# A mark set one granule later, and softmax portions counted twice, in a hybrid decoder block

## The chip, the cores and the metric

The kernel runs on one core of a Trainium2 chip. The metric is the device time of one execution in microseconds (us). Five instruction queues matter here: TensorE (PE, with its weight loads shown apart as PEld), VectorE (DVE), ScalarE (ACT), GpSimd (POOL) and SyncE (SP), which issues nearly all DMA transfers. Each queue runs its instructions in order; an instruction waits on semaphores for other engines.

## The reference

One decoder layer over 256 positions of 2048 channels in float32. The first half mixes three branches, the second is a gated feed-forward network.

```
h = rms_norm(x);  proj = h @ w_in            # a_in, b_in, q, kv, gates, merge gates
y_a = conformer_conv(a_in)                   # GLU, depthwise conv of 31, LayerNorm, swish, proj
y_b = chunked_spatial_gating(b_in)           # gelu, LayerNorm, 8 triangular 128x128 mixes, proj
y_c = native_sparse_attention(q, kv, gates)  # three attentions, see below, proj
mixed = (g_a * y_a + g_b * y_b + g_c * y_c) @ w_o
x = x + rms_norm(mixed)
h = rms_norm(x);  u = causal_dwconv3(h @ w_up)
x = x + rms_norm((silu(u_g) * u_v) @ w_down)
```

The sparse attention has 16 query heads in 4 groups, and three branches, each with keys and values of its own, added under gates:

```
kc = compress_blocks(k_cmp, pe_k, w1_k, w2_k)   # 15 blocks of 32 positions, a small MLP each
vc = compress_blocks(v_cmp, pe_v, w1_v, w2_v)
p_cmp = masked_softmax(q @ kc)                  # compressed branch: 15 keys
o_cmp = p_cmp @ vc
o_slc, o_win = ...                              # at 256 positions both see all earlier positions
o = gate0 * o_cmp + gate1 * o_slc + gate2 * o_win
```

## The kernel before

Every large product is made in three passes from a high and a low part of each operand. A weight piece of 128x1024 (512 KB) is fetched by SP into `wraw` (5 buffers, L106); ACT copies it rounded into `whi` (L146), and DVE subtracts to get `wlo` (L147), 4 buffers each. A *granule* is two such pieces. `mm_t` (L195 to L197) issues the three matmuls for one block of 128 input channels and 128 positions.

TensorE's main line is written in program order. The stage around the change is `branch(0, ...)`, the projection of the gating branch B: for each of four column blocks `cb` it makes the merge gates `pg` from four granules of `wt_g` (96 matmuls), evicts them through ACT as `mg` (Tanh, L1019), then makes `py` from two granules of `wt_p` (`q` is 0 and 1; 24 matmuls each, with `Bt` as the other operand), and DVE multiplies both into `mac` (L1044). `branch(1, ...)` does the same for branch A, with `At`.

Everything else runs in the background. Generators stand in a queue `bg`; `pump(ns)` is called after each granule, adds `ns` (6500 in this stage) to a running debt, and takes steps of the first generator while the debt is positive. Each step's `yield` says how many ns it is reckoned to cost.

```
    def pump(ns):
        debt[0] = min(debt[0], 0.0) + ns if not bg else debt[0] + ns
        while bg and debt[0] > 0:
            try:
                debt[0] -= next(bg[0])
            except StopIteration:
                bg.popleft()
```

So the yields decide only between which granules an operation is issued. A scheduler then places the instructions of each engine, by priorities and by its own reckoning of time, so that operations of one pump can move past neighbours.

In the queue, in this order, stand: the layer norm of branch A (`lna_gen`, which writes `At`, L514 to L520); `cmp_prep(0)`, which builds the compressed keys' operand `bk` (steps `bt`, L601, on DVE; L605 on ACT; L606 on DVE); `hold("outputs")`, which yields 6000 at each step until the mark "outputs" is set; `cmp_gen(0)`, the compressed keys: first product `zp` (L617, L619: 32 matmuls on four pieces of `w1`), then `hp` (L628) and `kcp` (L640); `cmp_prep(1)` and `cmp_gen(1)`, the same for the values, ending in `vcp` (L654) and `vbd` (L656); `cmp_attn(0)` and `cmp_attn(1)`, one compressed softmax for each half of the positions; and `attn`, eight attention units of the selected and window branches (scores `s`, transposes `pp`, values `O`).

`cmp_attn` issues scores `sc` (L716, PE), a masked softmax `ce` on DVE with one Exp on ACT (L727 to L739), in portions of 800, 800, 1300 and 100, and then a transpose `pcp` (L743, PE), copied out by ACT as `pct` (L745). The first attention units take `pct` at L825.

The mark "outputs" is set in `branch(0)` at `cb == 1`, after the first of the two `py` granules, just ahead of that granule's pump.

Of the kernel before, what the change touches and what calls it, by code (L numbers as in the profile page):

```python
# [56 lines left out]
def block(ctx: ExitStack, tc: tile.TileContext, x, xf, fp, cst, rows, sgw, w1, w2, wf_a, wt_bv, wf_bu, wf_c,  # L57
# [8 lines left out]
    marks = set()  # L66
# [12 lines left out]
    def bank(shape, name):  # L79
        return PB["pool"].tile(shape, F32, tag="bg", name=name)  # L80
# [7 lines left out]
    bg = deque()  # L88
    debt = [0.0]
# [8 lines that stand above are left out]
# [52 lines left out]
    def granule(src):  # L150
        return [piece(src[:, a:a + 1024], 1024) for a in (0, 1024)]
# [42 lines left out]
    def mm_t(ps, xh, xl, hi, lo, first, last):  # L194
        PE.matmul(ps, lhsT=xh, rhs=hi, start=first, stop=False)  # L195
        PE.matmul(ps, lhsT=xh, rhs=lo, start=False, stop=False)  # L196
        return PE.matmul(ps, lhsT=xl, rhs=hi, start=False, stop=last).ins  # L197

    def until(name):

        while name not in marks:
# [4 lines that stand above are left out]
# [43 lines left out]
    def q1(name, shape=(128, T)):  # L249
        return P1.tile(list(shape), F32, tag="q", bufs=12, name=name)  # L250
# [458 lines left out]

    Ct_box = {}  # L710

    def cmp_attn(qt):
        ps = bank([128, 2, 4, 2, 16], f"sc{qt}")
        for gg in range(2):
            for j in range(4):
                PE.matmul(ps[:, gg, j].rearrange("p r n -> p (r n)"), lhsT=qf[:, gg * 4 + j, qt * 128:qt * 128 + 128],  # L716
                          rhs=kcb[:, gg], start=True, stop=True)
        e = q1(f"ce{qt}", (128, 16, 16))
        psf = ps.rearrange("p g j r n -> p (g j r) n")
        m = P1.tile([128, 16], F32, tag="cm", name=f"cm{qt}")  # L720

        def bc(a):
            return a[:, None, :].to_broadcast([128, 16, 16])

        def bi(a):
            return a[:, :, None].to_broadcast([128, 16, 16])
        V.tensor_add(e, psf, bc(cs[:, K_CA + qt * 16:K_CA + qt * 16 + 16]))  # L727
        V.reduce_max(m, e, axis=AX.X)
        yield 800
        V.tensor_sub(e, e, bi(m))  # L730
        S.activation(e, e, AF.Exp)
        V.tensor_mul(e, e, bc(cs[:, K_C1 + qt * 16:K_C1 + qt * 16 + 16]))
        yield 800
        V.reduce_sum(m, e, axis=AX.X)
        V.tensor_scalar(m, m, TINY, None, op0=ALU.max)
        V.reciprocal(m, m)
        m4 = m.rearrange("p (g j r) -> p g j r", g=2, j=4)
        V.tensor_mul(m4, m4, gsg[:, qt, 0:16].rearrange("p (g r j) -> p g j r", g=2, r=2))
        V.tensor_mul(e, e, bi(m))  # L739
        yield 1300  # L740
        pp = bank([128, 2, 128], f"pcp{qt}")
        for gg in range(2):
            PE.transpose(pp[:, gg], e[:, gg * 8:gg * 8 + 8].rearrange("p a n -> p (a n)"), ident)  # L743
        pct[qt] = q1(f"pct{qt}", (128, 2, 128))
        S.activation(pct[qt], pp, AF.Copy)  # L745
        yield 100
# [127 lines left out]
            yield from u.values(O)  # L874

    for qt in range(2):
        bg.append(cmp_attn(qt))

    def alloc_C():
        Ct_box["t"] = s16(P1, [128, 8, 2, T], R, "Ct")  # L880
# [119 lines left out]
    def branch(bi, act_of):  # L1000

        for cb in range(4):
            pg = [PS.tile([128, 512], F32, tag="acc", name=f"pg{bi}{cb}{t}") for t in range(2)]
            for q in range(4):
                hs = granule(wt_g[(bi * 4 + cb) * 4 + q])
                for k in range(4 * q, 4 * q + 4):
                    hi, lo = hs[(k % 4) // 2]
                    c = slice((k % 2) * 512, (k % 2) * 512 + 512)
                    for t in range(2):
                        ts = slice(t * 128, t * 128 + 128)  # L1010
                        mm_t(pg[t], hT[:, k, 0, ts], hT[:, k, 1, ts], hi[:, c], lo[:, c], k == 0, k == KT - 1)
                if q < 3:
                    pump(BUDGET)
            tgs = {}
            for t in range(2):
                for a in range(2):
                    tgs[t, a] = q1(f"mg{bi}{cb}{t}{a}")
                    with tc.high_priority(offset=int(PR)):
                        gated[0] = S.activation(tgs[t, a], pg[t][:, a * 256:a * 256 + 256], AF.Tanh,  # L1019
                                                scale=rh[:, t:t + 1]).ins  # L1020
            marks.add("gates")
            pump(BUDGET)
            py = [PS.tile([128, 512], F32, tag="acc", name=f"py{bi}{cb}{t}") for t in range(2)]
            for q in range(2):
                hs = granule(wt_p[(bi * 4 + cb) * 2 + q])
                if cb == 0 and q == 0:
                    until("BA"[bi])
                act = act_of()
                for k in range(4 * q, 4 * q + 4):
                    hi, lo = hs[(k % 4) // 2]  # L1030
                    c = slice((k % 2) * 512, (k % 2) * 512 + 512)
                    for t in range(2):
                        ts = slice(t * 128, t * 128 + 128)
                        pe_last[0] = mm_t(py[t], act[:, k, 0, ts], act[:, k, 1, ts], hi[:, c], lo[:, c], k == 0, k == 7)
                if q == 0:
                    if cb == 1:
                        marks.add("outputs")
                    pump(BUDGET)
            for t in range(2):
                for a in range(2):  # L1040
                    cc = slice(cb * 512 + a * 256, cb * 512 + a * 256 + 256)
                    y = mac[:, t, cc] if bi == 0 else tgs[t, a]
                    with tc.high_priority(offset=int(PR)):
                        V.scalar_tensor_tensor(y, tgs[t, a], 1.0, py[t][:, a * 256:a * 256 + 256], op0=ALU.add,  # L1044
                                               op1=ALU.mult)
                        if bi:
                            V.tensor_add(mac[:, t, cc], mac[:, t, cc], y)
            pump(BUDGET)

    def mix_gen(cb):  # L1050

        for j in range(2 * cb, 2 * cb + 2):
# [10 lines left out]
            if j < NG:  # L1063
# [3 lines left out]
                mix["a", j] = a  # L1067

    branch(0, lambda: Bt_box["t"])
    branch(1, lambda: At)  # L1070
    until("A")
    until("C")
# [19 lines left out]
    for cp in range(2):  # L1092
# [20 lines left out]
        for n in range(2):  # L1113
            cb = 2 * cp + n
# [552 lines left out]
```

## Time and profile before

| | us |
|---|---|
| median of 3 runs | 1583.37 |
| lowest, highest | 1582.46, 1584.4 |
| the profiled execution's own time | 1584.43 |
| its span in the profile | 1582.7 |
| TensorE busy in the span | 1562.7 |
| VectorE busy | 1291.0 |
| ScalarE busy | 911.7 |

The profile is of one execution. A line of the timeline or of a group gives the start and duration, the engine, the source line, the operation, the tile written and the tiles read; a bracket at its end gives the idle time of that engine just before it and what released it. TensorE's matmuls overlap, so what one costs is read from one start to the next. The granted clock is 1.00 when TensorE runs at full speed.

### The profile page before, as it was taken

Reading aid. Unit: us, or ns where it says so; the run is one execution under the profiler, and the core shown is the slowest. Engines: PE = TensorE matmul, PEld = TensorE weight load, DVE = VectorE, ACT = ScalarE, POOL = GpSimd, SP = SyncE. Lnnn points to the kernel's source line nnn. Section 1 sums busy time; section 2 is a strip of 40 time slices with the busy share of each in tenths; the row PEclk is TensorE's granted clock in tenths of the full one; section 3 lists DMA queues with packets and bytes.
Section 4 is the critical chain, followed back from the end, with each engine's and each line's share of the span. In section 5 each row is a group of like instructions: output and inputs, shape, how many; then the busy total and the mean of one; then the engine's idle time right before and its main releaser. Section 6 shows DMA issues by size and latency. Waiting matters only on the chain.

```text
span 1582.7 us, 22435 instructions
## 1 busy us (share of the span) xinstructions
PE 1562.7 (99%) x8146; PEld 1325.7 (84%) x8146; DVE 1291.0 (82%) x2210; ACT 911.7 (58%) x1465; POOL 18.2 (1%) x46
## 2 busy tenths in 40 slices
PE   9999999998999999999999999999999999999997
PEld 7888899887777777888888888888888888888885
DVE  7899999878764554878887988888777777799898
ACT  7544544466476575556465655565555555556563
POOL 1000020000000000000000000000000000000000
PEclk9999999999999999999999999999999999999999
DMA  9555566666444546665784666666666666766672
GB/s 374 187 190 184 186 179 208 196 186 206 160 140 144 167 142 195 186 198 187 239 273 150 204 193 190 188 188 192 189 188 188 187 193 192 229 209 214 199 274 86
DMA packets 85440, 307.95 MB, mean 195 GB/s; under 512 B 9808, under 2 KB 10832, under 8 KB 84304
## 3 DMA queue, kind: packets, MB, share of 16 engines
q1 hardware_dynamic: 83952, 301.91, 60.1%
q0 software_dynamic: 944, 4.19, 0.8%
q8 instruction: 64, 1.05, 0.3%
q10 hardware_dynamic: 432, 0.41, 0.1%
q14 instruction: 48, 0.39, 0.1%
HBM read 301.23 MB, written 4.19 MB: 193 GB/s over the span
## 4 chain that ended last, share of the span: by engine, by line
PE 94%; DVE 3%; ACT 1%; issue 1%; DMA 0%; DVEq 0%; SPq 0%; ACTq 0%
PE ps L175 29%; PE ps L182 15%; PE pd0b L936 5%; PE pd1a L936 4%; PE pg L196 3%; PE pg L197 3%; PE pg L195 3%; PE py L196 3%; PE py L195 3%; PE py L197 2%; PE poa L936 2%; PE pg1a L936 2%; PE pg0a L936 2%; PE pd0a L936 2%; PE pd1b L936 1%; PE po L197 1%
## 5 line engine op out<-in xcount | busy, mean ns | idle before, releaser
L147 DVE TENSOR_TENSOR wlo<-wraw,whi 128x1024 fp32r<-128x1024 f32 (+1 forms) x376 | 457.1, 1218 | 98.7 <-ACT whi L146 92.0
L146 ACT ACTIVATE whi<-wraw 128x1024 fp32r<-128x1024 f32 (+1 forms) x376 | 393.5, 1052 | 153.2 <-PE pg L197 61.1
L175 PE MATMUL ps<-h2T,whi 128*128 128x512 f32 x1360 | 325.0, 391 | 0.0
L175 PEld LDWEIGHTS ps<-h2T,whi 128*128 128x128 f32 x1360 | 249.8, 188 | 48.2
L182 PEld LDWEIGHTS ps<-h2T,wlo 128*128 128x128 f32 x1360 | 174.5, 191 | 6.7
L182 PE MATMUL ps<-h2T,wlo 128*128 128x256 f32 x1360 | 176.6, 283 | 0.0
L175 PE MATMUL ps<-hT,whi 128*128 128x512 f32 x640 | 157.4, 392 | 0.0
L217 ACT ACTIVATE t<-ps 128x256 f32<-128x256 f32 x125 | 47.6, 382 | 187.0 <-PE ps L175 186.6
L901 DVE TENSOR_TENSOR wlowraw<-wraw,whiwraw 128x1024 fp32r<-128x1024 f32 x90 | 108.8, 1223 | 38.7 <-ACT whiwraw L901 37.2
L175 PEld LDWEIGHTS ps<-hT,whi 128*128 128x128 f32 x640 | 116.0, 189 | 21.2
L901 ACT ACTIVATE whiwraw<-wraw 128x1024 fp32r<-128x1024 f32 x90 | 94.7, 1057 | 49.2 <-PE py L197 17.4
L218 DVE TENSOR_TENSOR t<-ps,t 128x256 f32<-128x256 f32 x125 | 52.8, 423 | 70.3 <-ACT t L217 69.8
L478 DVE SCALAR_TENSOR_TENSOR cv<-hb,fps,cv 128x256 f32<-128x256 f32 x240 | 105.1, 479 | 0.2 <-ACT cv L474 0.2
L196 PE MATMUL pg<-wlo,hT 128*128 128x512 f32 x256 | 101.1, 395 | 0.4 <-DVE wlo L147 0.2
L197 PE MATMUL pg<-whi,hT 128*128 128x512 f32 x256 | 100.5, 393 | 0.0
L195 PE MATMUL pg<-whi,hT 128*128 128x512 f32 x256 | 98.7, 393 | 0.0
L182 PEld LDWEIGHTS ps<-hT,wlo 128*128 128x128 f32 x640 | 84.7, 190 | 4.7
L182 PE MATMUL ps<-hT,wlo 128*128 128x256 f32 x640 | 86.8, 283 | 0.0
L196 PEld LDWEIGHTS pg<-wlo,hT 128*128 128x128 f32 x256 | 48.1, 188 | 12.1 <-DVE wlo L147 1.2
L197 PEld LDWEIGHTS pg<-whi,hT 128*128 128x128 f32 x256 | 48.1, 188 | 10.3 <-issue 0.7
L195 PEld LDWEIGHTS pg<-whi,hT 128*128 128x128 f32 x256 | 47.9, 188 | 10.4 <-issue 0.7
L1388 ACT ACTIVATE fa<-fs,fps 128x256 f32<-128x256 f32 x88 | 52.5, 596 | 1.1 <-DVE fs L220 0.9
(1334 smaller groups left out, 2797.0 us busy)
## 6 DMA issues: line engine op xcount, KB each, us to landing
wraw<-in_wf_up_dram SPq DMA_DIRECT2D x176, 512.0 KB, 4.3
wraw<-in_wt_g_dram SPq DMA_DIRECT2D x64, 512.0 KB, 4.3
wraw<-in_wt_p_dram SPq DMA_DIRECT2D x48, 512.0 KB, 4.3
wraw<-in_wt_dn_dram SPq DMA_DIRECT2D x48, 512.0 KB, 4.4
wraw<-in_wf_a_dram SPq DMA_DIRECT2D x32, 512.0 KB, 4.4
wraw<-in_wt_gp_dram SPq DMA_DIRECT2D x20, 512.0 KB, 4.1
wraw<-in_wt_dq_dram SPq DMA_DIRECT2D x20, 512.0 KB, 4.5
qa<-in_wt_dq_dram SPq DMA_DIRECT2D x20, 512.0 KB, 4.1
```

Of the source, the lines that this page charges most:

```text
L146: S.activation(hi[:, :n], raw[:, :n], AF.Copy)
L147: V.tensor_sub(lo[:, :n], raw[:, :n], hi[:, :n].bitcast(F32))
L175: ins = PE.matmul(ps[:, :, ts], lhsT=ws[k // 8][0][:, c:c + 128], rhs=mov[:, k, :, ts], start=(k == 0 and not t), stop=(k == n - 1), skip_ ...
L182: ins = PE.matmul(ps[:, 1, ts], lhsT=ws[k // 8][1][:, c:c + 128], rhs=mov[:, k, 0, ts], start=False, stop=False, skip_group_check=True).ins
L195: PE.matmul(ps, lhsT=xh, rhs=hi, start=first, stop=False)
L196: PE.matmul(ps, lhsT=xh, rhs=lo, start=False, stop=False)
L197: return PE.matmul(ps, lhsT=xl, rhs=hi, start=False, stop=last).ins
L218: V.tensor_add(t1 if rb is not None else dst, ps[:, 0], t1)
L478: V.scalar_tensor_tensor(ca[:, j], hb[:, j, k:k + T], w(j, k), ca[:, j], op0=ALU.mult, op1=ALU.add)
L901: seq[eng] = [op(*args, **kw).ins]
L936: ins = PE.matmul(bank, lhsT=a[x], rhs=w[y], start=first and j == 0, stop=last and j == 2).ins
L1388: S.activation(a, s, AF.Identity, bias=fps[:, C_FB + f:C_FB + f + 1], scale=w[2])
```

## The change

Two edits, in the stage of `branch(0)`. The mark "outputs" is set after both `py` granules of `cb == 1` and not after the first, so that `hold` lets `cmp_gen(0)` start at the next pump, which comes behind the second granule. And each `cmp_attn` is wrapped in `apart`, which passes on its steps with twice the reckoned cost, so that one pump takes about half as much of them. No operation on the chip is added, dropped or changed in shape. Lines behind the new helper move down by 5.

```diff
     Ct_box = {}
 
+    def apart(work):
+
+        for ns in work:
+            yield 2.0 * ns
+
     def cmp_attn(qt):
...
     for qt in range(2):
-        bg.append(cmp_attn(qt))
+        bg.append(apart(cmp_attn(qt)))
...
                 if q == 0:
-                    if cb == 1:
-                        marks.add("outputs")
                     pump(BUDGET)
+            if cb == 1:
+                marks.add("outputs")
             for t in range(2):
                 for a in range(2):
                     cc = slice(cb * 512 + a * 256, cb * 512 + a * 256 + 256)
```

## The prediction

> **What bounds the kernel now.** I read the page first, then TensorE's waits, then the two places they point to.
>
> ```profile
> span 1582.7 us, 22435 instructions
> PE 1562.7 (99%) x8146; PEld 1325.7 (84%) x8146; DVE 1291.0 (82%) x2210; ACT 911.7 (58%) x1465; POOL 18.2 (1%) x46
> PE 94%; DVE 3%; ACT 1%; issue 1%; DMA 0%; DVEq 0%; SPq 0%; ACTq 0%
> ```
>
> TensorE sets the time: busy for 99% of the span, 94% of the chain. An edit that moves background work can only win where PE stands still or runs slowly, and can only lose by making it do so elsewhere. TensorE's own waits (engine, line, awaited: us in total, times, longest):
>
> ```profile
> PE zp L617 <- DVE bk L606: 4.0, 1, 4.0
> PE pcp L743 <- DVE ce L739: 3.0, 1, 3.0
> PE s L758 <- ACT pct L745: 0.5, 1, 0.5
> ```
>
> These three are nearly all of its waiting in mid-kernel, and they are what the edits move: zp is the compressed keys' first product, pcp the transpose that ends a compressed softmax, s the scores behind it. Windows of 1 us show what follows each wait (columns: length, busy time and count of PE, PEld, DVE, ACT and POOL, then the granted clock, DMA share, GB/s):
>
> ```profile
> 369.00:370.00 1.00, 1.00 (x6) 1.00 (x6) 0.50 (x2) 1.00 (x1) 0.14 (x2) 0.50 0.79 127
> 371.00:372.00 1.00, 1.00 (x11) 1.00 (x10) 0.51 (x2) 1.00 (x2) 0.00 (x0) 1.00 0.52 205
> 430.00:431.00 1.00, 1.00 (x7) 1.00 (x6) 1.00 (x9) 0.00 (x0) 0.00 (x0) 0.50 0.00 0
> 432.00:433.00 1.00, 1.00 (x7) 0.87 (x7) 1.00 (x7) 0.07 (x1) 0.00 (x0) 1.00 0.00 0
> ```
>
> After either wait PE works at a granted clock of 0.50, and is back at 1.00 by 371 and by 432. So each stall costs its idle time and a slow stretch. TensorE's timeline prices both:
>
> ```profile
> 362.65 0.39 PE L197 MATMUL py<-whi,Bt 128*128 128x512 f32 x1
> 367.08 0.58 PE L617 MATMUL zp<-whi,bk 128*128 128x256 f32 x1 [4.04 <-DVE bk L606]
> 370.61 0.28 PE L617 MATMUL zp<-whi,bk 128*128 128x256 f32 x1
> 372.50 0.63 PE L195 MATMUL py<-whi,Bt 128*128 128x512 f32 x2
> 377.99 1.00 PE L628 MATMUL hp<-sel,zs 128*128 128x64 f32 x8
> 378.79 0.71 PE L195 MATMUL pg<-whi,hT 128*128 128x512 f32 x2
> 385.31 0.33 PE L640 MATMUL kcp<-hid,w2s 128*128 128x64 f32 x2
> 403.20 1.87 PE L716 MATMUL sc<-kcb,qf 128*128 128x32 f32 x16
> 417.06 0.38 PE L743 MATMUL pcp<-idn,ce 128*128 128x128 f32 x2
> 417.27 1.87 PE L716 MATMUL sc<-kcb,qf 128*128 128x32 f32 x16
> 418.98 0.48 PE L195 MATMUL py<-whi,Bt 128*128 128x512 f32 x1
> 425.65 0.69 PE L743 MATMUL pcp<-idn,ce 128*128 128x128 f32 x2 [3.00 <-DVE ce L739]
> 426.81 2.08 PE L758 MATMUL s<-kkv,qf 64*128 64x128 f32 x16 [0.47 <-ACT pct L745]
> 432.11 0.48 PE L195 MATMUL pg<-whi,hT 128*128 128x512 f32 x1
> 436.61 1.16 PE L758 MATMUL s<-kkv,qf 64*128 64x128 f32 x16
> 437.70 0.50 PE L196 MATMUL pg<-wlo,hT 128*128 128x512 f32 x1
> 478.14 1.05 PE L825 MATMUL O<-pct,vbd 128*128 128x128 f32 x8
> 479.03 1.04 PE L816 MATMUL pp<-idn,ep 128*128 128x128 f32 x8
> ```
>
> Start-to-start prices at full clock: a granule of 24 py matmuls 377.99 - 372.50 = 5.49 us (0.229 each), a zp matmul (372.50 - 370.61) / 16 = 0.118, hp 0.80, sc 1.71, pcp 0.21, s 437.70 - 436.61 = 1.09, O for one group 0.89. The first 16 zp took 370.61 - 367.08 = 3.53 where 1.89 would do: the slow clock cost 1.64. From pcp to 432.11 there are 6.46 us, less the wait of 0.47 is 5.99, for 0.21 + 1.09 + 2 x 0.89 = 3.08 of work: 2.91 lost. So stall one is worth 4.04 + 1.64 = 5.7, stall two 3.00 + 0.47 + 2.91 = 6.4. No edit here can win much over 12 us.
>
> **Edit one: the mark "outputs" a granule later.** In the changed program's order of instructions the first 24 py matmuls of the second granule now stand ahead of the zp products, where before they stood behind them; no matmul is added. The weight splits of that granule take the places in the DVE and ACT queues that the zp weights had; SP fetches them in the new order too. The reason for the wait stays on DVE:
>
> ```profile
> 366.27 0.42 DVE L520 SCALAR_TENSOR_TENSOR At<-lz,At 128x256 fp32r<-128x256 f32 x1
> 366.60 0.76 DVE L606 TENSOR_TENSOR bk<-bt,bk 128x256 fp32r<-128x256 f32 x2
> 367.27 1.23 DVE L147 TENSOR_TENSOR wlo<-wraw,whi 128x1024 fp32r<-128x1024 f32 x1
> 368.74 0.76 DVE L606 TENSOR_TENSOR bk<-bt,bk 128x256 fp32r<-128x256 f32 x2
> 374.61 2.30 DVE L601 TENSOR_SCALAR bt<-kd,fps 128x60 f32<-128x60 f32 x12
> 376.81 1.23 DVE L147 TENSOR_TENSOR wlo<-wraw,whi 128x1024 fp32r<-128x1024 f32 x1
> 380.27 1.42 DVE L1044 SCALAR_TENSOR_TENSOR mac<-mg,py 128x256 f32<-128x256 f32 x4
> ```
>
> PE's last py before the wait starts at 362.65, so the granule runs from 362.88 to 368.37; bk's first two pieces land at 367.36, under it. The 4.04 us are covered and the clock stays up. What is late next is DVE: no row here has an idle time in brackets. From start to start an At takes 0.33, a wlo with an At 368.74 - 367.27 = 1.47, so a wlo 1.14; a bk pair 0.67; a bt 2.20 / 12 = 0.18; mac x4 about 1.33, its 1.42 less the 0.09 by which a next one overlaps. Its queue in the new order, after the bk pair that starts at 368.74: third zp split at 369.41 (lands 370.64); mac x4, fourth zp split at 371.88 (373.11); two pg splits (374.25, 375.39); a zp split for the values, 11 bt, another, 5 bt; then the split for pg's second granule at 380.52 (381.75). PE against it: 16 zp to 370.26, one more, wait 0.26; the group and one more zp to 371.58, two pg to 372.04, wait 1.07; 7 zp to 373.94, wait 0.31; 22 pg to 379.3, hp to 380.1, two pg to 380.55, wait 1.20; 22 pg to 386.79, kcp. New waits: 2.84 us in four pieces. Before, kcp came at 385.31 with 24 matmuls fewer behind it, which is 390.80 on the same footing. Edit one gains 4.0. (As a sum: 4.04 + 1.64, plus 1.03 of small losses between 378.79 and 385.31, where 24 matmuls took 6.52 instead of 5.49, less 2.84: 3.9.) Bounds: no DVE lag, 6.7; a lag twice as long, 1.0.
>
> **Edit two: softmax portions counted double.** No operation is added or removed; the yields weigh twice, so cmp_attn and all behind it in the queue spread over one more pump, and the order shows: 44 matmuls between sc(0) and pcp(0) (53 before), 32 between sc(1) and pcp(1) (15 before), then 18 more before s.
>
> ```profile
> 403.89 2.15 DVE L656 SCALAR_TENSOR_TENSOR vbd<-vcp,cs 128x128 f32<-128x128 f32 x8
> 425.17 0.42 DVE L739 TENSOR_TENSOR ce<-ce,cm 128x256 f32<-128x256 f32 x1
> 426.66 1.56 ACT L1019 ACTIVATE mg<-pg,rh 128x256 f32<-128x256 f32 x4
> L146 ACT ACTIVATE whi<-wraw 128x1024 fp32r<-128x1024 f32 (+1 forms) x376 | 393.5, 1052 | 153.2 <-PE pg L197 61.1
> ```
>
> The chain sc(1) to pcp(1) took 425.65 - 418.98 = 6.67 us of DVE and ACT behind 15 matmuls, 15 x 0.229 = 3.4 us. Now 32 matmuls give 7.3 us, and the order takes two wlo splits (2.3) out of the chain and puts mac x4 (1.33) in; ce's last step (425.17, 0.42) would be done some 1 to 2 us before PE asks. So pcp(1) is covered; pct is covered by the 18 matmuls behind it. In front of pcp(0) 44 matmuls, 10.1 us, stand against a chain like pcp(1)'s with the eight vbd ahead of it, 6.67 + 2.15 = 8.8. Who is delayed: mg x4 now stands right behind pct(0) on ACT, and the next pg needs the PSUM that mg's first two read. Since the last py, PE has pcp and sc to do, 1.92 us; ACT has a split (1.05), pct and two mg (1.56 / 4 = 0.39 each, pct taken as one), 2.2, and some 0.25 of handing over: PE waits about 0.55 us. Edit two gains 3.00 + 0.47 + 2.91 - 0.55 = 5.8. Bounds: with pcp(1) still late by half, 3; with the mg wait hidden, 6.4.
>
> **What is moved behind both.** The eight attention units start two pumps later and end 27 matmuls later, with 38 matmuls (8.7 us) still ahead of the next stage, so nothing of it hangs over. I put this at nothing: matmuls cover it.
>
> ```profile
> 440.00:500.00 60.00, 60.00 (x306) 46.83 (x305) 33.57 (x93) 41.49 (x111) 0.00 (x0) 1.00 0.52 158
> ```
>
> PE never waits in these 60 us, and DVE and ACT have 26 and 18 us free.
>
> **Sum.** 3.9 + 5.8 = 9.7 us. The profiled execution took 1584.43 (span 1582.7 and 1.7 around it), 1.06 over the median 1583.37 of the three runs; 9.7 off that median is 1573.7.
>
> [...] Half clock stood after an idle of 3.00 us (425.65). [...]
>
> **The rivals.**
> *The slow stretch belongs to the work, not the gap.* If 425.65 to 432.11 ran slowly because those are small matmuls, it stays slow when moved: gain 9.7 - 2.9 = 6.8, 1576.6. [...] Against it: s ran in 1.09 at 436.61, full clock. 5%.
> *The DVE lag is enough to slow the clock.* Four waits in 11 us might drop it as one of 4 us does; a slow stretch at half clock costs 1.6 (first) to 2.9 (second). Gain 6.8 to 8.1; 1576. Against it: no single wait is over 1.2 us. 8%.
> *One stall stays.* If pcp(1) is as late as before relative to PE, only edit one gains: 3.9, 1579.5. 4%.
> *It does not do what it says*, the lag eats edit one and the mg wait grows: no difference, 1583. 4%.
> *Slower: attention waits on its single pair of PSUM banks.* Scores and transposes of a unit share one two-bank buffer, so each transpose group waits for ACT's weights and each score group for ACT's eviction. If the two pumps push units into stretches where ACT also has mg and the splits, each of 8 units could hold PE. It decides from (9.7 + 3.2) / 8 = 1.6 us a unit; at 2 us a unit, 16 - 9.7 = 6 us slower, 1589.5. Against it: the 60.00 of 60 above, and ACT's free 18 us. 11%.
>
> **How the numbers follow.** Likeliest: both stalls go, 68%, 1573.7, its own range 1571 (no lag) to 1576.5 (lag twice as long). Taking in the two clock cases brings in 81%, less the tails of each; I go on to 1579.5 for the stall that stays, and down to 1570.8. Outside are the no-change and slower cases and thin tails. About 0.2%, 3.2 us, can be told from no change here: faster 68 + 5 + 8 + 4 = 85%, within 4%, slower 11%.
>
> **What would show it.** In the new trace: PE's waits no longer name bk or ce; instead about four waits for wlo, 2 to 3.5 us in sum, near 370 to 382; granted clock 1.00 from 360 to 440; pcp(1) without a wait; a short wait of pg for mg near 418; the first pg behind O some 10 us earlier than the old 432.11 plus 50 matmuls. I am wrong if a wait over 2.5 us stands between 360 and 440, or if PE idles in the attention units.

## The result and the profile after

The changed kernel takes 1574.71 us (median of 5 runs, 1574.34 to 1575.46), the kernel before 1583.37 (5 runs, 1582.46 to 1584.4): a ratio of 0.9947, 95% interval 0.9932 to 0.9961, or 8.7 us less. The forecast was 1573.7. The profiled execution took 1574.36, its span is 1572.7. The head of its page:

```profile
span 1572.7 us, 22434 instructions
PE 1558.4 (99%) x8146; PEld 1322.0 (84%) x8146; DVE 1289.9 (82%) x2210; ACT 911.2 (58%) x1465; POOL 18.2 (1%) x46
```

The span is 10.0 us shorter at the same 8146 matmuls; PE's busy time fell by 4.3 us, since matmuls at half clock count as longer (a zp matmul 0.41 us before, at half clock, and 0.28 at full). TensorE's waits, all of the view:

```profile
PE warm L287 <- POOL wz L284: 1.4, 1, 1.4
PE zp L619 <- DVE wlo L147: 1.0, 2, 0.8
PE pg L196 <- DVE wlo L147: 0.8, 1, 0.8
PE pv L401 <- ACT swraw L117: 0.4, 1, 0.4
PE pg L195 <- ACT mg L1024: 0.3, 1, 0.3
PE pd1a L941 <- DVE wloq_4b L906: 0.2, 1, 0.2
```

No wait names bk, ce or pct any more; in their place stand short waits for weight splits and one for mg. From L712 on the new kernel's lines are 5 higher: pcp is L748, s L763, O L830. The rows of TensorE's timeline that answer to those of before:

```profile
367.89 0.28 PE L617 MATMUL zp<-whi,bk 128*128 128x256 f32 x1
370.33 0.39 PE L619 MATMUL zp<-wlo,bk 128*128 128x256 f32 x1 [0.26 <-DVE wlo L147]
372.79 0.38 PE L619 MATMUL zp<-wlo,bk 128*128 128x256 f32 x1 [0.78 <-DVE wlo L147]
381.39 0.50 PE L196 MATMUL pg<-wlo,hT 128*128 128x512 f32 x1 [0.82 <-DVE wlo L147]
386.51 0.33 PE L640 MATMUL kcp<-hid,w2s 128*128 128x64 f32 x2
418.56 0.50 PE L195 MATMUL pg<-whi,hT 128*128 128x512 f32 x1 [0.27 <-ACT mg L1024]
426.00 0.38 PE L748 MATMUL pcp<-idn,ce 128*128 128x128 f32 x2
430.44 1.16 PE L763 MATMUL s<-kkv,qf 64*128 64x128 f32 x16
431.53 2.05 PE L830 MATMUL O<-pct,vbd 128*128 128x128 f32 x16
433.34 0.47 PE L196 MATMUL pg<-wlo,hT 128*128 128x512 f32 x1
```

The first zp and pcp(1) have nothing in brackets; s takes 1.09 from start to start and both O groups 1.81, the prices of full clock. The first pg behind O starts at 433.34 where before it stood at 432.11 with 50 matmuls still to come: 432.11 + 50 x 0.229 = 443.56, so 10.2 us earlier, where some 10 were forecast. Two windows hold the two places:

```profile
370.00:380.00 10.00, 8.92 (x49) 7.32 (x49) 10.00 (x26) 5.60 (x10) 0.00 (x0) 1.00 0.85 284
420.00:430.00 10.00, 10.00 (x47) 8.20 (x46) 6.76 (x17) 3.88 (x5) 0.00 (x0) 1.00 0.27 92
```

Granted clock 1.00 in both: the slow stretches went with the stalls. Not all of the 10.0 us of span is the change's: the anchor rows lie 0.4 to 0.5 us earlier than before already ahead of the first edited instruction (the py that would follow 362.65 starts at 362.88 before; here 24 py matmuls, 24 x 0.229 = 5.49, precede 367.89, so it starts at 362.40). The medians' 8.7 is the fairer number.

### The profile page after: what moved, and what is told of

Same layout as the page of the kernel before. It is cut to its first block, busy times and chain, and to the rows that moved or that the text cites. A ratio compares the mean times of both kernels' runs of the same rounds, so it can differ in the third digit from the quotient of the medians.

```text
span 1572.7 us, 22434 instructions
## 1 busy us (share of the span) xinstructions
PE 1558.4 (99%) x8146; PEld 1322.0 (84%) x8146; DVE 1289.9 (82%) x2210; ACT 911.2 (58%) x1465; POOL 18.2 (1%) x46
## 4 chain that ended last, share of the span: by engine, by line
PE 94%; DVE 3%; ACT 1%; issue 1%; DMA 0%; DVEq 0%; SPq 0%; ACTq 0%
PE ps L175 29%; PE ps L182 15%; PE pd0b L941 5%; PE pd1a L941 4%; PE pg L197 3%; PE pg L196 3%; PE pg L195 3%; PE py L196 3%; PE py L195 3%; PE py L197 3%; PE poa L941 2%; PE pg1a L941 2%; PE pg0a L941 2%; PE pd0a L941 2%; PE pd1b L941 1%; PE po L195 1%
```

## The experiments

**One edit at a time.** The prediction gave each edit a gain of its own, 4.0 and 5.8. But in the order of instructions only the two together put more work ahead of pcp(1): between sc(1) and pcp(1) stand 15 matmuls before, none with the mark alone, 15 with the weight alone, 32 with both. The mark alone:

```diff
-        bg.append(apart(cmp_attn(qt)))
+        bg.append(cmp_attn(qt))
```

> Only the mark is set a granule later; the softmax portions count as before. Theory A (the prediction's sum: two edits, each worth its own stall): the zp stall and its slow clock go as in the changed kernel, pcp(1) stays as it was, gain 4.0 us, about 1579.4. Theory B (the edits work only together, since what covers pcp(1) is how many matmuls fall between the two halves of the second softmax): in this kernel's order no matmul at all stands between sc(1) and pcp(1), where the kernel before had 15, so the wait there grows from 3.0 us to about 4.5 (the chain took 4.9 us in the changed kernel, with 1.3 of it for mac, which is not in it here) and the clock falls after it: gain 4.0 - 1.5 = 2.5, about 1580.9. A wait of 3.0 at pcp would speak for A, one over 4 for B.

It took 1582.06 us (11 runs), ratio 0.999, interval 0.9981 to 0.9999: 1.4 us gained. Two of its waits, and rows of its timeline:

```profile
PE zp L619 <- DVE wlo L147: 1.0, 2, 0.8
PE pcp L748 <- DVE ce L744: 4.3, 1, 4.3
```

```profile
423.20 0.69 PE L748 MATMUL pcp<-idn,ce 128*128 128x128 f32 x2 [4.31 <-DVE ce L744]
424.37 2.08 PE L763 MATMUL s<-kkv,qf 64*128 64x128 f32 x16 [0.47 <-ACT pct L750]
426.38 3.60 PE L830 MATMUL O<-pct,vbd 128*128 128x128 f32 x16
```

Stall one is gone, as forecast. Stall two has grown from 3.00 to 4.31 us, since no matmul is left to cover the second softmax: some 3.4 us of cover are gone (15 x 0.229), while the softmax on DVE lost two weight splits (2.3 us) from its middle. And s and O still run slowly: s took 2.01 us from start to start (424.37 to 426.38) for the 1.09 of full clock, and the granted clock was 0.50 from 422.83 to 429.66. With the mark worth some 3 us (below) and a wait 1.3 longer, 1.7 would be left; 1.4 was measured.

The weight alone:

```diff
                 if q == 0:
+                    if cb == 1:
+                        marks.add("outputs")
                     pump(BUDGET)
-            if cb == 1:
-                marks.add("outputs")
```

> Only the softmax portions count double; the mark is set where it was. Theory A: pcp(1) is covered, the zp stall of 4.0 us stays, gain 5.8 us, about 1577.6. Theory B: the order has the same 15 matmuls between sc(1) and pcp(1) as before, so both stalls stand as they were: no difference, 1583.4, with waits of 4.0 at zp and 3.0 at pcp.

It took 1583.65 us (11 runs), ratio 1.0, interval 0.9991 to 1.0009: nothing. Its two large waits:

```profile
PE zp L617 <- DVE bk L606: 4.0, 1, 4.0
PE pcp L748 <- DVE ce L744: 3.0, 1, 3.0
```

Both old stalls, to the tenth. One edit gained 1.4, the other nothing, both 8.7: the split of the sum into 4.0 and 5.8 was wrong.

**What edit two needs.** Is the mark itself needed for stall two, or only a pump boundary inside the second softmax, wherever it comes from? With the mark where it was and a weight of 2.5, the order puts 57 matmuls between sc(1) and pcp(1):

```diff
-            yield 2.0 * ns
+            yield 2.5 * ns
...
                 if q == 0:
+                    if cb == 1:
+                        marks.add("outputs")
                     pump(BUDGET)
-            if cb == 1:
-                marks.add("outputs")
```

> The mark stays where it was before the change; the yields of the two compressed softmaxes are weighted 2.5 instead of 2. In the order of instructions 57 matmuls then stand between sc(1) and pcp(1) (15 before, 15 with the weight 2 and the old mark, 32 with the whole change), since a pump boundary falls inside the second softmax. Theory A (what decides stall two is whether a pump boundary falls inside the second softmax; the mark matters only by where it sets that boundary): pcp(1) has no wait, the clock stays at 1.00 from 420 to 440, zp still waits 4.0 us for bk with its slow stretch; gain 5.5 to 6.4, median 1577.0 to 1578. Theory B (stall two also needs the weight splits that the moved mark takes out of the DVE queue): pcp(1) still waits over 1 us, median over 1580.

1577.36 us (5 runs), ratio 0.9962, interval 0.9948 to 0.9975, against 1583.86 for the kernel before beside it: 6.5 us gained. From its timeline of TensorE:

```profile
362.51 0.39 PE L197 MATMUL py<-whi,Bt 128*128 128x512 f32 x1
366.95 0.39 PE L617 MATMUL zp<-whi,bk 128*128 128x256 f32 x1 [4.05 <-DVE bk L606]
384.25 0.33 PE L640 MATMUL kcp<-hid,w2s 128*128 128x64 f32 x2
430.96 0.38 PE L748 MATMUL pcp<-idn,ce 128*128 128x128 f32 x2
436.06 1.16 PE L763 MATMUL s<-kkv,qf 64*128 64x128 f32 x16
```

Stall one stands as before, stall two is gone, and no weight split had to leave the DVE queue for it. So it is the boundary that covers stall two; in the change, the weight of 2 makes it only because the mark has moved the softmax one granule on.

**The whole change with a weight of 3.** It puts 53 matmuls ahead of pcp(0) and 48 ahead of pcp(1), and pushes the attention's end further back.

```diff
-            yield 2.0 * ns
+            yield 3.0 * ns
```

> The whole change with the weight 3 in place of 2: 53 matmuls in front of pcp(0), 48 in front of pcp(1) (44 and 32), so no softmax can be late, and the attention ends beyond the point where the next stage's first matmuls start. By the prediction's step (what is moved behind costs nothing as long as matmuls stand ahead of the next stage): the compressed part as in the changed kernel or 0.3 us better, but at the end about what the mark one block later showed, 1.4 us of waiting of pg0b for Ct: 1575 to 1576.5. By the rival that the attention units themselves become slower where they are moved: several waits inside the units and 1579 or more. If the end is covered: 1574.5.

1574.24 us (5 runs, 1574.14 to 1574.67), ratio 0.9941, interval 0.9929 to 0.9954: no different from the change by what can be told here. The wait for Ct (the tile with the attention's result, copied out of the PSUM of O) that was expected did not come, nor did any in the attention units; in mid-kernel only the waits for weight splits are left (0.24, 0.78 and 0.82 us). From its timeline:

```profile
368.57 0.28 PE L617 MATMUL zp<-whi,bk 128*128 128x256 f32 x1
387.17 0.33 PE L640 MATMUL kcp<-hid,w2s 128*128 128x64 f32 x2
624.69 1.94 PE L763 MATMUL O<-ep,kkv 128*64 128x512 f32 x8
636.71 0.39 PE L941 MATMUL pg0b<-whig00a,hT 128*128 128x512 f32 x1
```

The last O now stands among the next stage's first matmuls, but still starts 12 us ahead of pg0b, the first to take a PSUM bank that the attention had: no wait shows at that distance.

This kernel and the one with the weight of 2.5 alone differ in the mark and in the weight, but both cover stall two, and TensorE's waits in them differ at stall one only. So they also price the mark: counted from the py that follows the first granule, which starts at 368.57 - 5.49 = 363.08 here and would start at 362.51 + 0.23 = 362.74 with the weight of 2.5, kcp comes 24.09 us later here, and 21.51 + 5.49 = 27.00 there, where 24 matmuls are still to come. The mark is worth 2.9 us; the medians say 1577.36 - 1574.24 = 3.1.

**The mark another granule on.** Does a still later mark win the rest, by giving DVE more time?

```diff
-            if cb == 1:
-                marks.add("outputs")
...
                     pump(BUDGET)
+            if cb == 1:
+                marks.add("outputs")
```

> As the changed kernel, but the mark is set behind the pump that ends the column block, one pump later still. If VectorE's lag is what is left of the first stall (waits of 0.26, 0.78 and 0.82 us for wlo), another granule of matmuls ahead of zp gives it time: these waits and the 0.27 for mg shrink, gain up to 2.1 us more, 1572.6. Against that, the last attention unit now ends 50 matmuls behind the start of the next stage, which needs its PSUM banks; if that is no longer hidden, PE waits there and the time is 1576 or more.

1577.85 us (5 runs, 1575.97 to 1579.69), ratio 0.9967, interval 0.9955 to 0.998: 3.1 us worse than the change. Its timeline shows what going later costs:

```profile
387.67 0.50 PE L196 MATMUL pg<-wlo,hT 128*128 128x512 f32 x1 [2.15 <-DVE wlo L147]
636.54 1.94 PE L763 MATMUL O<-ep,kkv 128*64 128x512 f32 x8
639.91 0.50 PE L941 MATMUL pg0b<-whig00a,hT 128*128 128x512 f32 x1 [1.42 <-DVE Ct L842]
```

The short waits at zp are gone, but DVE's lag gathers into one wait of 2.15 us (after one of 0.75 us for the copies on ACT), behind which the clock fell to 0.50 for 3.4 us, and the attention's last O now starts 3.4 us ahead of pg0b, which waits for the copy of the last O into Ct.

**DVE's lag taken away.** The shifted pieces for the values' half, bt, go to GpSimd:

```diff
-                V.tensor_scalar(tmp[:, i, :, 0:15], kd_t[:, kv, :, ...
+                (G if kv else V).tensor_scalar(tmp[:, i, :, 0:15], kd_t[:, kv, :, ...
```

> As the changed kernel, but the 16 bt additions for the compressed values are issued on GpSimd and no longer on VectorE (2.9 us of its queue between 376 and 380). If VectorE's queue is what PE waits for at the split for pg's second granule, that wait of 0.82 us goes and the waits ahead of it (0.26, 0.78) stay: gain 0.8 us more, 1573.9. If GpSimd is slow enough that bk comes late, PE waits at the values' zp instead and the time is 1575 or more.

1575.06 us (5 runs, 1574.46 to 1576.47). The 0.82 us of pg for its split did go, and no wait for the values' bk came up, but the forecast gain of 0.8 us does not show: so small a wait is within the spread of executions. With the weight 3 beside it:

> The whole change with the weight 3, and the shifted key pieces for the values' half (bt) computed on GpSimd instead of VectorE. The weight 3 alone left waits of 0.24 and 0.78 us of zp and 0.82 us of pg for weight splits and gave 1574.24; with GpSimd the 0.82 went in the changed kernel. If DVE's lag is what is left: 1573.4 (0.8 us less). If GpSimd's slower work turns up elsewhere, as it did there (1575.06 against 1574.71): 1574.2 to 1574.6. In both cases the difference is about that between two executions of one kernel.

1574.08 us (5 runs, 1573.6 to 1574.95), ratio 0.9942, interval 0.9928 to 0.9955: the fastest median of all and not told apart from 1574.24 or 1574.71. With 1.0 us of zp and 0.2 us of pg left in its waits, nothing that can be measured is left at these places.

**The clock.** What idle halves it? Six pauses in the changed kernel's second branch, matmuls of 128x512 behind each:

```diff
+    SITES = {(2, 'g', 1): 0, (2, 'g', 3): 2, (2, 'p', 0): 3, (3, 'g', 1): 4, (3, 'g', 3): 5, (3, 'p', 0): 8}
+    def gap(n, after):
...
+        V.tensor_copy(c[:, 0:128], z)
+        V.tensor_copy(c[:, 128:256], z)
+        for _ in range(n):
+            V.tensor_add(c, c, c)
...
+        return PE.transpose(z2, c[:, 0:128], ident).ins
```

> The changed kernel with six pauses of TensorE put in on purpose in the second branch, at its third and fourth column blocks: a transpose, a chain of DVE copies and 0, 2, 3, 4, 5 or 8 additions on 128x256, a second transpose, and the matmuls there held in their written order; the output is not altered. Each addition is about 0.4 us, so idle times of about 1 to 4 us. Theory A (an idle of some length near 3 us, whatever the work behind it, halves the clock): the granted clock is 0.50 for some 3 to 6 us after the pauses of 3 us and over, and 1.00 after those up to 1.2 us; what lies between is open. [...] Rival (the slow stretch belongs to the small matmuls of zp and of pcp, s and O): no pause slows the clock, as here the matmuls behind are 128x512. Time: the sum of the pauses, about 14 us, and 1.6 to 2.9 us for each slow stretch: 1590 to 1600.

The pauses idled 0.38, 2.63, 3.18, 3.64, 4.10 and 5.48 us, and all but the first were followed by half clock. The time, 1630.14 (median of two), is far over the expected 1590 to 1600: the held order made the attention units wait as well (O and pp for ep: 12.5 us), and the pauses summed to 19. The use of the run is the clock. Read in windows of 1 us, the falls lie at 609.44, 619.68, 640.16, 657.22 and 667.46: 3, 6, 5 and 3 times 3.413 us apart. Windows laid on that grid (length, then busy time of PE first; the clock is third from the end):

```profile
606.03:609.44 3.41, 1.33 (x7) 1.12 (x8) 1.98 (x3) 1.89 (x5) 0.00 (x0) 1.00 0.57 190
609.44:612.85 3.41, 3.41 (x10) 2.64 (x9) 0.00 (x0) 0.21 (x1) 0.00 (x0) 0.50 0.29 113
612.85:616.27 3.42, 2.81 (x13) 2.01 (x11) 1.76 (x4) 1.53 (x2) 0.00 (x0) 1.00 0.17 20
```

In these three rows the clock follows one window behind PE: the one with 1.33 us busy has full clock and is followed by a whole one at 0.50; PE fills that one, and the next is at 1.00. Shorter pauses (the same kernel with other counts):

```diff
-    SITES = {(2, 'g', 1): 0, (2, 'g', 3): 2, (2, 'p', 0): 3, (3, 'g', 1): 4, (3, 'g', 3): 5, (3, 'p', 0): 8}
+    SITES = {(2, 'g', 1): 1, (2, 'g', 3): 0, (2, 'p', 0): 1, (3, 'g', 1): 0, (3, 'g', 3): 1, (3, 'p', 0): 0}
```

> The kernel of the longer pauses, with 1, 0, 1, 0, 1 and 0 additions in place of 0 to 8: by the longer pauses (2.63 us with two additions, 3.18 with three, 3.64 with four) these idle about 2.2 and 1.75 us. In the longer pauses every change of the granted clock lay on one grid of 3.41 us, and a window of that grid with 2.08 us of idle in it was followed by one at 0.50, while one with 1.48 us was not. Theory (more than about half a window of idle, 1.7 us, in one window of a grid that runs on by itself): pauses of 1.75 us slow nothing, or hardly one; pauses of 2.2 us slow the clock only where they fall into one window, that is in about one case of three, and each slow stretch is 3.41 us long. Rival (the length of the pause alone decides, at somewhere between 1.5 and 2.6 us): all three pauses of 2.2 us do the same.

The one execution took 1609.81 us. The pauses came out shorter than meant, 1.0 to 1.1 and 0.4 us, so neither theory was tried as written. One place answers all the same: a unit's wait of 1.43 us and a pause of 1.04 fell into one window.

```profile
595.90 0.33 PE L1011 MATMUL gz<-idn,mac 128*128 128x128 f32 x1 [1.43 <-DVE Ct L842]
597.27 0.34 PE L1020 MATMUL gy<-idn,gc 128*128 128x128 f32 x1 [1.04 <-DVE gc L1017]
```

```profile
587.22:590.63 3.41, 1.53 (x12) 1.05 (x10) 0.00 (x0) 1.75 (x4) 0.00 (x0) 1.00 0.00 0
590.63:594.04 3.41, 2.94 (x8) 0.77 (x8) 0.00 (x0) 0.42 (x1) 0.00 (x0) 0.50 0.00 0
594.04:597.45 3.41, 0.94 (x5) 0.32 (x4) 1.60 (x4) 0.60 (x1) 0.57 (x1) 1.00 0.42 137
597.45:600.86 3.41, 3.41 (x10) 2.64 (x10) 0.00 (x0) 0.00 (x0) 0.00 (x0) 0.50 0.42 171
```

No single idle was over 1.43 us, and the clock fell. The weight of 2.5 alone gives the other bound; its window at the start of stall one was busy for 1.59 us, and the next one kept full clock; that one, busy for 1.17, was followed by half clock:

```profile
361.30:364.71 3.41, 1.59 (x8) 0.97 (x6) 3.41 (x18) 3.41 (x10) 0.00 (x0) 1.00 0.62 209
364.71:368.12 3.41, 1.17 (x10) 1.17 (x11) 3.41 (x8) 1.83 (x5) 0.26 (x2) 1.00 0.29 60
368.12:371.53 3.41, 3.41 (x19) 3.41 (x18) 3.20 (x6) 2.28 (x3) 0.25 (x2) 0.50 0.75 244
```

So in these runs the clock went by the busy time in a window of the grid, and not by the length of one idle. Of the windows at full clock that were laid on the grid in the kernel before and in six of the runs, the 14 with 1.53 us of PE or less (0.00 to 1.53) were all followed by half clock, and of those with 1.94 or more none was; between them there is no order: the 1.59 above kept full clock, and one of 1.69 in the kernel with the shorter pauses, with score products of the attention units, lost it (0.50 from 570.15 on):

```profile
566.73:570.15 3.42, 1.69 (x14) 1.10 (x14) 2.06 (x9) 0.60 (x1) 0.00 (x0) 1.00 0.01 2
```

## Why the prediction was right, and where not

**What bounds the kernel: right.** The gain came from TensorE's two stalls and their slow stretches alone; the rest of its timeline moved as a block: 10.2 us at the first pg behind O, 10.05 at the next stage's first matmul (pg0a, 634.36 before and 624.31 after), 10.0 at the end.

**The total: right, its division among the edits wrong.** The order of the whole change, 32 matmuls between sc(1) and pcp(1), was put down to edit two. That is the step that failed: the order of each edit alone would have shown 0 and 15. The total did not suffer from it, as both parts were worked out in the order of the whole change. The stalls as such were sized well: taking stall two away alone gained 6.5 us (6.0 against the 1583.4 of the other rounds) where the prediction had 6.4 for it (5.8 after the wait for mg); taking stall one away gained 2.9 to 3.1 where it had 4.0.

**Edit one's 4.0.** In the two profiled executions it is 385.31 + 5.49 - 362.88 = 27.92 less 386.51 - 362.40 = 24.11, or 3.8. But 0.7 to 0.9 of this was that one execution of before: the same stretch is 27.25 with the weight of 2 alone and 27.00 with 2.5, which have the same order up to kcp, stall one included. The 1.03 of "small losses between 378.79 and 385.31" was taken for a part of the stall and is mostly chance: these 24 matmuls took 6.52 us there and 5.89 and 5.61 in the other two. One wait in it, which the prediction did not name, is in the execution of before alone:

```profile
379.75 0.50 PE L196 MATMUL pg<-wlo,hT 128*128 128x512 f32 x1 [0.25 <-DVE wlo L147]
```

**Why 8.7 and not 9.7.** Between the two profiled executions the sum came as forecast: 10.2 at the first pg behind O, less the 0.5 that was there ahead of the edits, is 9.7. But the stalls were priced in an execution that took 1.06 us more than its median, and their price was taken off the median; and the profiled execution of after lies 0.35 under its own. What the priced execution has above others is in the small losses, and in the slow stretch of stall two. With the weight of 2 alone, and the same matmuls in the same order, the stretch from pcp to pg lost 430.25 - 424.85 - 0.47 - 3.08 = 1.85 us to the slow clock, and not 2.91:

```profile
424.85 0.44 PE L748 MATMUL pcp<-idn,ce 128*128 128x128 f32 x2 [3.00 <-DVE ce L744]
430.25 0.48 PE L195 MATMUL pg<-whi,hT 128*128 128x512 f32 x1
```

That execution took 1582.58 us and the one that was priced 1584.43. So these two terms are sized for a slow execution, and too high for the median.

**The walk through DVE's queue: nearly right.** Forecast were waits of 0.26, 1.07, 0.31 and 1.20 us, counted from where a matmul could start to where it does. Counted so, the timeline has 0.42 (369.91 to 370.33), 0.96 (371.83 to 372.79), 0.20 (373.72 to 373.92) and 1.07 (380.32 to 381.39), in sum 2.65 for 2.84. The brackets are lower, 0.26, 0.78, none and 0.82, since they hold only the time in which PE was idle. From the start of the second granule to kcp it took 24.11 us for the forecast 386.79 - 362.88 = 23.91.

**Edit two's chain: right for the whole change.** The last step of the second softmax on DVE ended with time to spare, and pg was held up for mg by 0.42 us (416.43 + 1.71 = 418.14 to 418.56; 0.27 of it idle) for the forecast 0.55. The "0.25 of handing over" in that forecast answers to two steps in the execution of before, from pcp to pct on ACT, 417.47 - 417.27 = 0.20, and pct (done at 426.38 + 0.38 = 426.76) to s, 426.81 - 426.76 = 0.05:

```profile
417.47 0.38 ACT L745 ACTIVATE pct<-pcp 128x256 f32<-128x256 f32 x1 [1.15 <-PE pcp L743]
426.38 0.38 ACT L745 ACTIVATE pct<-pcp 128x256 f32<-128x256 f32 x1 [2.58 <-PE pcp L743]
```

The end of the second softmax in the changed kernel:

```profile
423.19 0.42 DVE L744 TENSOR_TENSOR ce<-ce,cm 128x256 f32<-128x256 f32 x1
```

It is done at 423.61, 2.4 us before pcp(1) at 426.00; forecast were 1 to 2.

**What is moved behind: right.** Nothing in the attention units waits, with the weight 2 or 3; it costs 1.42 us, with the mark another granule on, where the last O comes within 3.4 us of pg0b. In the changed kernel PE is through with the last O at 615.52, 8.8 us ahead of the next stage's first matmul, for the forecast 8.7. The slower rival, units held by their PSUM pair, did not happen: in the window that was quoted of before, PE has no idle in the changed kernel either.

```profile
440.00:500.00 60.00, 60.00 (x310) 46.60 (x307) 35.08 (x107) 45.23 (x122) 0.00 (x0) 1.00 0.51 158
```

**The clock rivals.** That the slow stretch belongs to the small matmuls fell: s and O ran at full prices in the changed kernel, and the pauses slowed matmuls of 128x512. That DVE's short waits would slow it did not happen here, though waits of 1.43 and 1.04 us within one window of 3.41 us were followed by half clock in the kernel with the shorter pauses (0.50 from 597.45 to 600.86). In the changed kernel the waits of 0.26 and 0.78 us, 2.5 us apart, left PE busy for 2.37 us in a window that holds both, and the next was at 1.00; so was the stretch with the 0.82:

```profile
369.41:372.82 3.41, 2.37 (x17) 1.72 (x15) 3.41 (x7) 2.52 (x3) 0.00 (x0) 1.00 0.77 241
372.82:376.24 3.42, 3.38 (x17) 2.79 (x18) 3.42 (x5) 1.78 (x4) 0.00 (x0) 1.00 0.71 219
376.00:390.00 14.00, 13.18 (x77) 11.31 (x76) 11.49 (x30) 7.84 (x14) 0.00 (x0) 1.00 0.82 271
```

**One stall stays.** This rival is what either edit alone does (1582.06 and 1583.65), though not the change.

## What to carry to other kernels

When two edits share a queue of background work, make the order of instructions for each alone before giving each its share: a boundary that one edit moves can be what makes the other work, or undo it. Count the matmuls that stand between the last product that feeds a softmax and the first that needs it; here 15 cost 3.00 us, none 4.31, and 32 nothing. A price that is read in one execution belongs to that execution's time: take it off that time and not off the median, and put a loss that only one execution shows into the range.

## What the runs showed of the hardware

In the traces of this case the falls of the granted clock lay whole steps of 3.413 us apart, 3, 6, 5 and 3 of them in the kernel with pauses. In the windows laid on this grid, 1.53 us of PE and under were followed by half clock, 1.94 and over were not. Products of 128x512 ran at half clock after such a window as the small ones did (with the pauses, py at 611.12 to 612.40 took 0.43 us from start to start, and 0.23 from 613.08 on). A whole slow window of back-to-back matmuls cost 1.64 us in stall one (3.53 us for 1.89 of work). In the profiled execution of before, windows on its grid (17 steps of 3.413 us lie between the two falls, 367.11 and 425.14):

```profile
421.73:425.14 3.41, 0.92 (x5) 0.42 (x3) 3.04 (x7) 1.06 (x1) 0.00 (x0) 1.00 0.41 133
425.14:428.55 3.41, 2.42 (x18) 2.03 (x18) 2.49 (x8) 1.84 (x5) 0.00 (x0) 0.50 0.57 174
428.55:431.96 3.41, 3.41 (x18) 3.19 (x17) 3.41 (x22) 0.83 (x2) 0.00 (x0) 0.50 0.00 0
```

Stall two cost two slow windows there. In the profiled execution of the weight alone, with the same idle of 3.00 us, the grid lay elsewhere and it cost one (425.79 to 429.20). The same stall thus had two prices, 2.91 and 1.85 us lost behind the wait. For the way back the numbers are others: the windows at half clock with 0.54 (667.46 to 670.87 with the pauses), 2.42 (in the rows above) and 2.56 us of PE (422.83 to 426.24 with the mark alone) were each followed by another slow one, those with 2.72 us or more (2.72 at 640.16 to 643.57 in the kernel with pauses) by full clock. Whether the shape of the products has a part in it was not shown.
